# VectorE order, a resident residual and split attention outputs in a one-core hybrid encoder layer

## The chip, the cores and the metric

The kernel runs on one core of a Trainium2 chip. The metric is the device time of one execution, in microseconds (us). The engines are TensorE (PE in the profile, its weight loads PEld), VectorE (DVE), ScalarE (ACT), GpSimd (POOL) and SyncE (SP), whose queue issues nearly all DMAs.

## The reference

One layer of a streaming encoder on 512 prompt frames and 8 x 16 sample frames, 640 tokens of width 1024, in float32:

```python
x = x + 0.5 * swiglu(rmsnorm(x, ffn1_norm), ffn1_wgu, ffn1_wd)      # d_ff 2816
cols = rmsnorm(x, mix_norm) @ w_in
ret_cols, mla_cols, ssm_cols = split(cols)
o_ret = retention(rope(q), rope(k), v) normed, * silu(gate)         # 8 heads of 64
o_mla = latent_attention(c_q 384, c_kv 256, k_rope 32)              # 8 heads, softmax, chunk-causal
o_ssm = rmsnorm((ssd_scan(conv(xbc), dt, a) + d * xs) * silu(z))    # 16 heads of 64, state 128
x = x + concat([o_ret, o_mla, o_ssm]) @ w_out                       # 2048 x 1024
x = x + 0.5 * swiglu(rmsnorm(x, ffn2_norm), ffn2_wgu, ffn2_wd)
```

The sample frames attend to a cache of 256 earlier frames for each of 8 streams (latents `ckv` and a rotary key `krope`), and start from given retention, state-space and convolution states. The outputs are x, the new latents and keys, and the new states.

## The kernel before

Tokens lie on the free axis in five tiles of 128 (`NT` = 5, `T` = 640, `H2` = 320); the 1024 channels are eight tiles of 128 partitions (`NK` = 8). Every large product is done in three passes: each operand is split into a rounded high part (ScalarE's copy to the fast float32 format) and the rest (VectorE's subtraction), and TensorE multiplies high by high, low by high and high by low. `part(h, l, src)` is that split for data (L382, L383); `wunit` splits a loaded weight block `wr` into `wh` (L290) and `wl` (L291).

Stages in order of time: first feed-forward (`ffn("1", ...)`), input projection in units (`tok_first`, `tok_unit`, each with a sink that empties the PSUM bank), attention over the prompt, attention of the samples over the caches (`sample_a` and what follows it), retention and convolution, the state-space scan in five token blocks with the sample steps between, the output projection `wout` in two halves (`woa` for retention and attention, `wos` for the state space), and the second feed-forward. The code is written stage by stage; a scheduler sorts each engine's instructions by priorities (`prio`, and `urgent()` for the highest), and `tc.issue_after` binds an instruction behind another. On each engine the instructions run in the sorted order. SP's DMAs run in its queue's order, so a store that waits holds the loads behind it.

**The feed-forward** multiplies 2 x 2 blocks with seven products in place of eight. For each of four pairs of channel tiles, `blocks(q)` splits the plain blocks and `sums(q)` makes four sums of blocks (L415 to L418) and splits those; `squares(q, eng)` adds the squares of x for the norm (L430). The first two hidden tiles use plain products (L466), the others the seven-product form (L556). `statistics()` turns the squares into the token norms (`norm_stats`, L361, L363) and spreads them into a row tile R (`spread`, L371, L372). R multiplies the gate before and after the silu (`plain_gate` L541, L543; `scaled_silu` L523, L525); L599 is the down projection. In the first feed-forward, `cache_norms` (L682 to L719) prepares the cached keys on the side, with a chain of a reciprocal square root (L265 to L272) at its end.

**Small features.** The unit `winc` makes 176 columns a token: 128 of c_q, 16 of dt and 32 of the rotary key. Its sink (`sink_c`) empties one of two PSUM banks `pd` on two engines: ScalarE takes c_q (L860), VectorE takes dt (`dtr`, L861) and the key (`kr`, L862).

**Attention outputs.** `mix_out` transposes an output tile, copies it to `mo` and stores it in DRAM: `ma_dr` for retention and attention, `ms_dr` for the state space (L920 to L924). Before the output projection `mix_in` loads those as `mraw` and splits them (L1684 to L1687). `sample_a(b)` loads the cached latents of stream b twice, as `c_t` (columns by tokens, L1130) and `c_n` (tokens by columns, L1131), into three buffers.

**Retention** rotates q and k in `ro` with three VectorE instructions (L1286 to L1288) and three GpSimd ones (L1289 to L1291).

**State space.** Decay factors come from a pool with `DECB` = 6 buffers; each block's sample steps load their inputs into `st` and copy them into `sr` (L1616, L1618).

**Output projection.** `sink_x` loads a half row of the residual from `x_dr` into `xc`, adds the PSUM bank (L1701) and stores it to `y_dr`; after the first half all eight rows are loaded again, on GpSimd's queue, into `xres`, to which the second half adds.

Of the kernel before, what the change touches and what calls it, by code (L numbers as in the profile page):

```python
# [197 lines left out]
def body(tc, a):  # L198
# [182 lines left out]
    def part(h, l, src):  # L381
        S.copy(h, src)  # L382
        V.tensor_sub(l, src, h.bitcast(F32))  # L383

    class Tokens:
# [473 lines left out]
    def sink_c(t, ps):  # L859
        S.activation(cqt[:, t, 256:384], ps[:, :128], AF.Copy, scale=rstd[:, t:t + 1])  # L860
        V.scalar_tensor_tensor(dtr[:, t, :], ps[:, 128:144], rstd[:, t:t + 1], rowp[:, R_DTB:R_DTB + 16], op0=ALU.mult, op1=ALU.add)  # L861
        V.tensor_scalar_mul(kr[:, t, :], ps[:, 144:176], rstd[:, t:t + 1])  # L862
# [895 lines left out]
```

## Time and profile before

| | |
|---|---|
| time, median of 3 runs | 1654.43 us (1651.13 to 1659.39) |
| profiled execution | 1650.01 us, span 1648.2 us |
| mean granted TensorE clock | 0.973 |
| busy: TensorE, VectorE, ScalarE, GpSimd | 1603.1, 1128.2, 697.6, 384.0 us |
| DMA | 178.32 MB, 108 GB/s on the mean |

The profile is of one execution, taken by the hardware profiler, and its times count from the first instruction. A row of a timeline gives start, duration, engine, line, operation, output and inputs; a row of a group gives count, busy time and mean in ns. "PEclk" is the clock that TensorE was granted, as a share of full speed. A busy TensorE is not TensorE at full speed: at a clock of 0.5 it is as busy and does half the work.

### The profile page before, as it was taken

To read this page: it belongs to the slowest core of one execution; us is meant where nothing else is said; L and a number is where in the kernel's file an instruction comes from. 1 tells how busy PE (TensorE), PEld (TensorE's weight loads), DVE (VectorE), ACT (ScalarE), POOL (GpSimd) and SP (SyncE) were. 2 spreads that over 40 slices of the span, in tenths; PEclk is the share of its full clock that TensorE was granted. 3 is DMA by queue.
4 is the path that set the end of the run, shared out by engine and by line. 5 is a ranking of instruction groups with operands and counts; after the bars stand their busy time and mean duration, and the time that the engine had idled before them with its cause. 6 is when DMAs were issued, how large, how long until landed. Compare 5 with 4: busy or idle time off the path is not lost.

```text
span 1648.2 us, 27379 instructions
## 1 busy us (share of the span) xinstructions
PE 1603.1 (97%) x10867; PEld 1541.1 (93%) x10867; DVE 1128.2 (68%) x1790; ACT 697.6 (42%) x1282; POOL 384.0 (23%) x396
## 2 busy tenths in 40 slices
PE   8999999999999999999989998999999999999998
PEld 8999999999999999986989996689999999999998
DVE  8788777777573472563689757755678977777762
ACT  6554333333353334553333365433445433343430
POOL 3422222222201000002142224341004422223220
PEclk8999999999997999998999998799999999999999
DMA  4332222222151333113144547677312322222221
GB/s 179 103 94 80 78 88 79 80 87 77 52 203 51 114 99 120 64 42 106 56 146 141 169 144 224 203 235 243 119 46 71 103 77 90 78 79 88 77 77 65
DMA packets 88316, 178.32 MB, mean 108 GB/s; under 512 B 13352, under 2 KB 48072, under 8 KB 87996
## 3 DMA queue, kind: packets, MB, share of 16 engines
q1 hardware_dynamic: 86012, 171.14, 32.9%
q10 hardware_dynamic: 1536, 2.82, 0.6%
q0 software_dynamic: 640, 2.62, 0.5%
q8 instruction: 85, 1.39, 0.4%
q14 instruction: 43, 0.35, 0.1%
HBM read 143.45 MB, written 33.10 MB: 107 GB/s over the span
## 4 chain that ended last, share of the span: by engine, by line
PE 86%; DVE 7%; DMA 4%; issue 2%; ACT 1%; POOL 1%; SPq 0%; DVEq 0%; ACTq 0%; POOLq 0%
PE bank L556 29%; PE pair L599 19%; PE pd L820 12%; PE pd L1662 6%; PE pd L1395 2%; PE pair L466 1%; PE pair L696 1%; PE p L1082 1%; DVE wl L291 1%; PE po L1104 1%; DVE ac L1409 1%; PE pb L1576 1%; PE bank L466 1%; PE ps L1630 1%; DMA mraw<-ms_dr 1%
## 5 line engine op out<-in xcount | busy, mean ns | idle before, releaser
L291 DVE TENSOR_TENSOR wl<-wr,wh 128x1024 fp32r<-128x1024 f32 (+3 forms) x161 | 202.6, 1259 | 52.0 <-ACT wh L290 48.3
L290 ACT CAST wh<-wr 128x1024 fp32r<-128x1024 f32 (+3 forms) x161 | 163.0, 1015 | 171.9 <-PE pair L599 73.3
L599 PE MATMUL pair<-xh,wh 128*128 128x320 f32 x672 | 206.8, 310 | 1.4 <-ACT xh L382 1.0
L599 PE MATMUL pair<-xl,wh 128*128 128x320 f32 x672 | 207.3, 309 | 0.0
L599 PE MATMUL pair<-xh,wl 128*128 128x320 f32 x672 | 207.2, 309 | 0.0
L523 POOL TENSOR_TENSOR gt<-gt,R 128x320 f32<-128x320 f32 x82 | 93.7, 1143 | 481.8 <-DVE gt L583 441.3
L556 PE MATMUL bank<-xsh,wh 128*128 128x320 f32 x656 | 203.0, 310 | 2.3 <-ACT s L560 2.3
L556 PE MATMUL bank<-xsh,wl 128*128 128x320 f32 x656 | 203.3, 310 | 0.0
L556 PE MATMUL bank<-xsl,wh 128*128 128x320 f32 x656 | 203.2, 310 | 0.0
L601 DVE SCALAR_TENSOR_TENSOR x<-pair,x 128x640 f32<-128x640 f32 x96 | 78.7, 822 | 149.9 <-PE pair L599 149.8
L820 PE MATMUL pd<-wh,xh 128*128 128x256 f32 (+1 forms) x560 | 166.5, 297 | 5.3 <-DVE kr L862 3.3
L820 PE MATMUL pd<-wl,xh 128*128 128x256 f32 (+1 forms) x560 | 166.5, 297 | 0.0
L820 PE MATMUL pd<-wh,xl 128*128 128x256 f32 (+1 forms) x560 | 166.2, 297 | 0.0
L525 POOL TENSOR_TENSOR gt<-gt,R 128x320 f32<-128x320 f32 x82 | 118.1, 1442 | 72.6 <-ACT gt L524 72.6
L599 PEld LDWEIGHTS pair<-xh,wh 128*128 128x128 f32 x672 | 125.7, 188 | 2.3 <-ACT xh L382 1.3
L556 PEld LDWEIGHTS bank<-xsh,wh 128*128 128x128 f32 x656 | 123.6, 189 | 3.0 <-ACT s L560 2.6
L599 PEld LDWEIGHTS pair<-xl,wh 128*128 128x128 f32 x672 | 126.2, 188 | 0.1
L599 PEld LDWEIGHTS pair<-xh,wl 128*128 128x128 f32 x672 | 126.1, 188 | 0.0
L556 PEld LDWEIGHTS bank<-xsl,wh 128*128 128x128 f32 x656 | 123.7, 189 | 0.4
L556 PEld LDWEIGHTS bank<-xsh,wl 128*128 128x128 f32 x656 | 123.8, 189 | 0.2
L820 PEld LDWEIGHTS pd<-wh,xh 128*128 128x128 f32 x560 | 112.5, 201 | 8.4 <-issue 5.8
L820 PEld LDWEIGHTS pd<-wl,xh 128*128 128x128 f32 x560 | 112.4, 201 | 3.5 <-issue 3.3
(568 smaller groups left out, 4127.6 us busy)
## 6 DMA issues: line engine op xcount, KB each, us to landing
wr<-in_wgu SPq DMA_DIRECT2D x88, 512.0 KB
wr<-in_wd SPq DMA_DIRECT2D x40, 512.0 KB
wr<-in_wint SPq DMA_DIRECT2D x28, 512.0 KB
wr<-in_winx SPq DMA_DIRECT2D x12, 512.0 KB
qk_dr<-stg SPq DMA_DIRECT2D x40, 128.0 KB
wr<-in_woa SPq DMA_DIRECT2D x8, 512.0 KB
hb<-in_sssm SPq DMA_DIRECT2D x16, 256.0 KB
out_ssms<-hb SPq DMA_DIRECT2D x16, 256.0 KB
```

The lines of the kernel that those rows point to most:

```text
L290: S.copy(hv, raw)
L291: V.tensor_sub(lv, raw, hv.bitcast(F32))
L466: PE.matmul(out[gu][hf], w_, x_, start=q == 0 and k == 0 and i == 0, stop=q == 3 and k == 1 and i == 2)
L523: G.tensor_mul(gt[:, hf], gt[:, hf], R3[:, hf])
L525: G.tensor_mul(gt[:, hf], gt[:, hf], R3[:, hf])
L556: PE.matmul(out, w_[:, o:o + P], x_[:, PSLOT[p]], start=start and k == 0 and i == 0, stop=k == 3 and i == 2, skip_group_check=not start)
L599: PE.matmul(pt[:, hf, :H2], w_[:, o:o + P], x_[:, hf * H2:(hf + 1) * H2], start=j == 0 and i == 0, stop=j == g - 1 and i == 2)
L601: V.scalar_tensor_tensor(xv, pt[:, :, :H2], 0.5, xv, op0=ALU.mult, op1=ALU.add)
L696: PE.matmul(pt[:, kt], x_[:, o:o + P], w_[cc][:, :512], start=c == 0, stop=c == 5)
L820: PE.matmul(ps[:, :w], x_[k][:, t * P:(t + 1) * P], w_[:, k * w:(k + 1) * w], start=c == 0, stop=c == 23)
L1395: PE.matmul(ps[:, :H2], w_[:, o:o + P], x_[k][:, hf * H2:(hf + 1) * H2], start=c == 0, stop=c == 23)
L1662: PE.matmul(ps[:, :H2], w_[:, o:o + P], x_[k][:, hf * H2:(hf + 1) * H2], start=k == 0 and i == 0, stop=k == NK - 1 and i == 2)
```

## The change

1. In the first feed-forward the block work of all four pairs comes first, then all sums, then all squares (bound with `issue_after`); the squares and the plain gates' two products move from GpSimd to VectorE. How many pieces of the previous group's down projection go between the units of the second group becomes 0, 2, 3, 3.
2. `sink_c` empties the bank with one ScalarE copy of 176 columns; one GpSimd copy and one VectorE addition take `kr` and `dtr` from there for all five tiles.
3. The attention outputs are split where they are made (`mix_split`) and stored as two parts (`mh_dr`, `ml_dr`), which are loaded straight into `xh`, `xl`.
4. The first cache uses the buffer that held the keys, and its loads go ahead of the attention stores.
5. Retention's three GpSimd instructions go to VectorE.
6. `sr` is loaded without `st`; `DECB` is 5.
7. The residual is loaded into `xres` before the output projection and stays there; `xc`, `y_dr` and the reload go. R of the mixer, `stg` and `mo` get pools that close at other places.

```diff
             part(h[:, 0], l[:, 0], b1[:, 0])
             part(t[:, 0], t[:, 1], b1[:, 1])
-            part(h[:, 1:3], l[:, 1:3], b2)
+            self.last = part(h[:, 1:3], l[:, 1:3], b2)
...
-            with urgent():
+            with urgent(), tc.issue_after(tok.last.ins):
                 for q in range(4):
-                    tok.squares(q, G)
+                    tok.sums(q)
+            with urgent(), tc.issue_after(tok.last.ins):
+                for q in range(4):
+                    tok.squares(q, V)
...
         def plain_gate(gt, ut):
-            G.tensor_mul(gt, gt, R3)
+            V.tensor_mul(gt, gt, R3)
             S.activation(gt, gt, AF.Silu)
-            G.tensor_mul(gt, gt, R3)
+            V.tensor_mul(gt, gt, R3)
...
-    DECB = 6
+    DECB = 5
...
     def sink_c(t, ps):
-        S.activation(cqt[:, t, 256:384], ps[:, :128], AF.Copy, scale=rstd[:, t:t + 1])
-        V.scalar_tensor_tensor(dtr[:, t, :], ps[:, 128:144], rstd[:, t:t + 1], rowp[:, R_DTB:R_DTB + 16], op0=ALU.mult, op1=ALU.add)
-        V.tensor_scalar_mul(kr[:, t, :], ps[:, 144:176], rstd[:, t:t + 1])
+        S.activation(cqt[:, t, 256:432], ps[:, :176], AF.Copy, scale=rstd[:, t:t + 1])
         S.activation(junk()[:, :128], cqt[:, t, 256:384], AF.Square, accum_out=cqs[:, 1, t:t + 1])
...
+    G.tensor_copy(kr, cqt[:, :, 400:432])
+    V.tensor_add(dtr, cqt[:, :, 384:400], brow(rowp[:, R_DTB:R_DTB + 16], NT))
...
+    def mix_split(src, k0, n, t, where):
+        pt = turn()
+        for i in range(n):
+            PE.transpose(pt[:, i * P:(i + 1) * P], src[:, i * P:(i + 1) * P], ident)
+        h, l = (where.tile([P, n, P], F32R, tag=s, name=nm(s), bufs=2) for s in ("moh", "mol"))
+        pv = pt[:, :n * P].rearrange("p (f t) -> p f t", f=n)
+        S.copy(h, pv)
+        V.tensor_sub(l, pv, h.bitcast(F32))
+        Q.dma_start(out=mh_dr[:, k0:k0 + n, t * P:(t + 1) * P], in_=h.bitcast(F32))
+        Q.dma_start(out=ml_dr[:, k0:k0 + n, t * P:(t + 1) * P], in_=l.bitcast(F32))
...
         def sample_a(b):
-            c_t = t1_.tile([P, 2, 272], F32, tag="c_t", name=nm("c_t"), bufs=3)
-            c_n = t1_.tile([P, 2, CKV], F32, tag="c_n", name=nm("c_n"), bufs=3)
+            if b == 0:
+                kt_ = m0.tile([P, 1600], F32, tag="K", name=nm("K"))
+                c_t, c_n = kt_[:, 0:544].rearrange("p (c n) -> p c n", c=2), kt_[:, 544:1056].rearrange("p (c n) -> p c n", c=2)
...
-        G.tensor_mul(ro[:, :, 32:64], x1, sn)
-        G.tensor_mul(tb, x2, cs)
-        G.tensor_add(ro[:, :, 32:64], ro[:, :, 32:64], tb)
+        V.tensor_mul(ro[:, :, 32:64], x1, sn)
+        V.tensor_mul(tb, x2, cs)
+        V.tensor_add(ro[:, :, 32:64], ro[:, :, 32:64], tb)
...
         def sample_load(b):
-            st = sb.tile([P, 1280], F32, tag="st", name=nm("st"), bufs=STKB)
+            sr[0] = sb.tile([P, 1280], F32R, tag="sr", name=nm("sr"), bufs=SRB)
             for o in range(2):
-                Q.dma_start(out=st[64 * o:64 * o + 64], in_=xw_dr[b + o])
-            sr[0] = sb.tile([P, 1280], F32R, tag="sr", name=nm("sr"), bufs=SRB)
-            S.copy(sr[0], st)
+                Q.dma_start(out=sr[0][64 * o:64 * o + 64].bitcast(F32), in_=xw_dr[b + o])
...
+    xres = [None] * NK
+    for k in range(NK):
+        xres[k] = x2p.tile([P, T], F32, tag=f"x{k}", name=nm("x2"))
+        Q.dma_start(out=xres[k], in_=x_dr[k])
...
     def sink_x(d, cs, ps):
-        xc = wp.tile([P, H2], F32, tag="xc", name=nm("xc"))
-        Q.dma_start(out=xc, in_=x_dr[d][:, cs])
-        V.tensor_add(xc, ps, xc)
-        Q.dma_start(out=y_dr[d][:, cs], in_=xc)
+        V.tensor_add(xres[d][:, cs], ps, xres[d][:, cs])
```

VectorE at the opening, before. `xh_26` is the first pair's lower tile, `xh_29` the second pair's; L383 splits a block, L400 scales a tile, L415 to L418 are sums, L291 splits weights.

```order
L415 TENSOR_TENSOR xh_26_171<-xh_26_171 128x320
L400 TENSOR_SCALAR xh_27_172<-x_5_105,colp 128x640
L291 TENSOR_TENSOR wl_151<-wr_148,wh_150 128x1024
L416 TENSOR_TENSOR xh_26_171<-xh_26_171,xh_27_172 128x320
L383 TENSOR_TENSOR xsl_118<-xh_27_172,xsh_119 128x640
L291 TENSOR_TENSOR wl_158<-wr_155,wh_157 128x1024
L400 TENSOR_SCALAR xh_30_183<-x_6_106,colp 128x640
L417 TENSOR_TENSOR xh_27_172<-xh_27_172,xh_26_171 128x320
L383 TENSOR_TENSOR xsl_118<-xh_26_171,xsh_119 128x640
L400 TENSOR_SCALAR xh_33_194<-x_7_107,colp 128x640
L418 TENSOR_TENSOR xh_27_172<-xh_27_172 128x320
L383 TENSOR_TENSOR xsl_116<-xh_29_182,xsh_117 128x320
```

After, with its own line numbers (L381 splits, L398 scales, L413 is the first sum, L289 splits weights):

```order
L381 TENSOR_TENSOR xsl_115<-xh_29_182,xsh_116 128x320
L381 TENSOR_TENSOR xl_31_186<-xh_29_182,xl_31_186 128x320
L398 TENSOR_SCALAR xh_33_194<-x_7_106,colp 128x640
L381 TENSOR_TENSOR xsl_115<-xh_30_183,xsh_116 128x640
L381 TENSOR_TENSOR xsl_113<-xh_32_193,xsh_114 128x320
L398 TENSOR_SCALAR xh_36_205<-x_8_107,colp 128x640
L381 TENSOR_TENSOR xl_34_197<-xh_32_193,xl_34_197 128x320
L381 TENSOR_TENSOR xsl_113<-xh_33_194,xsh_114 128x640
L381 TENSOR_TENSOR xsl_111<-xh_35_204,xsh_112 128x320
L381 TENSOR_TENSOR xl_37_208<-xh_35_204,xl_37_208 128x320
L381 TENSOR_TENSOR xsl_111<-xh_36_205,xsh_112 128x640
L413 TENSOR_TENSOR xh_26_171<-xh_26_171 128x320
```

Before, the four sums of the first pair stand between its blocks and those of the second; after, the first sum comes behind the blocks of the fourth.

VectorE around the end of the cache keys' chain (`ivc` is its result) and the small features, before (`pd` are the PSUM banks):

```order
L291 TENSOR_TENSOR wl_5435<-wr_5432,wh_5434 128x1024
L272 SCALAR_TENSOR_TENSOR ivc<-rit_5406,riy_5404 128x128
L861 SCALAR_TENSOR_TENSOR dtr<-pd_5048,rstd,rowp 128x16
L862 TENSOR_SCALAR kr<-pd_5048,rstd 128x32
L861 SCALAR_TENSOR_TENSOR dtr<-pd_5078,rstd,rowp 128x16
L862 TENSOR_SCALAR kr<-pd_5078,rstd 128x32
```

After:

```order
L268 TENSOR_TENSOR rit_5405<-rit_5405,rih_5404 128x128
L289 TENSOR_TENSOR wl_5434<-wr_5431,wh_5433 128x1024
L270 SCALAR_TENSOR_TENSOR ivc<-rit_5405,riy_5403 128x128
L289 TENSOR_TENSOR wl_5440<-wr_5437,wh_5439 128x1024
L289 TENSOR_TENSOR wl_5586<-wr_5583,wh_5585 128x1024
L873 TENSOR_TENSOR dtr<-cqt,rowp 128x80
L875 TENSOR_TENSOR cqs<-cqs 128x5
```

No instruction that empties a `pd` bank of this unit stands behind the chain any more. ScalarE, which now empties them alone (L862):

```order
L859 ACTIVATE jnk_5041,cqs<-cqt 128x256
L862 ACTIVATE cqt<-pd_5055,rstd 128x176
L863 ACTIVATE jnk_5081,cqs<-cqt 128x128
L862 ACTIVATE cqt<-pd_5083,rstd 128x176
L863 ACTIVATE jnk_5109,cqs<-cqt 128x128
```

SP's queue at the start of the samples' attention, before:

```order
L924 DMA ma_dr<-mo_6857 128x2x128
L924 DMA ma_dr<-mo_6917 128x2x128
L924 DMA ma_dr<-mo_6985 128x2x128
L924 DMA ma_dr<-mo_7061 128x2x128
L1130 DMA c_t_7133<-in_ckvT 128x2x256
L924 DMA ma_dr<-mo_7122 128x2x128
L1131 DMA c_n_7134<-in_ckvN 128x512
L1130 DMA c_t_7167<-in_ckvT 128x2x256
L1131 DMA c_n_7168<-in_ckvN 128x512
```

After:

```order
L891 DMA qk_dr_4829<-stg_8456 128x256
L1150 DMA K_7156<-in_ckvT 128x2x256
L1151 DMA K_7156<-in_ckvN 128x512
L936 DMA mh_dr<-moh_6632 128x2x128
L937 DMA ml_dr<-mol_6633 128x2x128
```

and further on in the same queue:

```order
L936 DMA mh_dr<-moh_7078 128x2x128
L937 DMA ml_dr<-mol_7079 128x2x128
L936 DMA mh_dr<-moh_7142 128x2x128
L937 DMA ml_dr<-mol_7143 128x2x128
L1150 DMA c_t_7187<-in_ckvT 128x2x256
L1151 DMA c_n_7188<-in_ckvN 128x512
```

The first cache (now in buffer `K`) stands ahead of all attention stores, the second behind all sixteen; before, the first stood ahead of the last of eight and the second behind it.

On TensorE the instructions are the same in number and shape; 373 matmuls instead of 326 (the warm-up's left out) stand ahead of the first L599, and 396 of the output projection's 768 instead of 506 behind the last transposes of the state-space stage.

More of the change, by code (lines that the diff above doesn't have):

```diff
@@ L419, in sums @@
             part(h[:, 3:5], l[:, 3:5], b1)
-            part(h[:, 5:7], l[:, 5:7], b2)
+            self.last = part(h[:, 5:7], l[:, 5:7], b2)
         def squares(self, q, eng):
@@ L615, in ffn @@
             acts = []
-            per = 8 // g
             for j in range(g):
+                per = (0, 2, 3, 3)[j] if first and gi == 1 else 8 // g
                 if f < npl:
@@ L621, in ffn @@
                         uts = [plain_gate(*u) for u in raw_out]
-                        with urgent():
-                            for q in range(4):
-                                tok.sums(q)
                         for i in range(2):
@@ L723, in body @@
     with ExitStack() as st:
+        r1 = pool(st, "R1", side="right")
         xp = pool(st, "x1", side="right")
@@ L728, in body @@
         tok.open((0, 1, 2, 3))
-        ffn("1", tok, True, False, bank, pair, R)
+        ffn("1", tok, True, False, bank, pair, r1.tile([P, T], F32, tag="R", name="R"))
         prio(10)
@@ L784, in body @@
     stg_st = ExitStack()
-    stg = pool(stg_st, "stg", 4)
+    stg = pool(stg_st, "stg", 4, side="right")
+    R_st = ExitStack()
+    R = pool(R_st, "Rm", side="right").tile([P, T], F32, tag="R", name="Rm")
     dtr = keep.tile([P, NT, SH], F32, tag="dtr", name="dtr")
@@ L795, in body @@
     xs_dr = [tc.dram_tile([P, 1024], F32, name=f"xs_dr{t}") for t in range(NT)]
-    ma_dr = tc.dram_tile([P, NK, T], F32, name="ma_dr")
+    ma_dr = tc.dram_tile([P, 4, T], F32, name="ma_dr")
+    mh_dr, ml_dr = (tc.dram_tile([P, 4, T], F32, name=n) for n in ("mh_dr", "ml_dr"))
     MSC = (0, 384, T)
@@ L852, in body @@
     t0 = pool(mt_st, "mt0")
-    cqt = t0.tile([P, NT, CQ], F32, tag="cqt", name="cqt")
+    cqt = t0.tile([P, NT, CQ + 48], F32, tag="cqt", name="cqt")
     def sink_a(t, ps):
@@ L945, in body @@
         for t in range(NT):
-            cq = cqt[:, t, :]
+            cq = cqt[:, t, 0:CQ]
             S.activation(cq, cq, AF.Copy, scale=cqr[:, t:t + 1])
@@ L1048, in prep @@
         def prep(u):
-            K = ub.tile([P, 16, 96], F32, tag="K", name=nm("K"))
+            K = m0.tile([P, 1600], F32, tag="K", name=nm("K"))[:, 0:1536].rearrange("p (a d) -> p a d", a=16)
             Vv = ub.tile([P, 4, 256], F32, tag="Vv", name=nm("Vv"), bufs=2)
@@ L1193, in body @@
         ret_unit(u)
+    for u in range(ZPRE):
+        tok_unit(a["wint"][2 + u], 256, silu_sink(z_dr, 256 * u))
+    mog_st = ExitStack()
+    mog = pool(mog_st, "mog", 2)
     ssd_st = ExitStack()
@@ L1469, in body @@
         tok_unit(a["wint"][2 + u], 256, silu_sink(z_dr, 256 * u))
+    stg_st.close()
+    x2p = pool(x2_st, "x2", side="right")
     wo_st = ExitStack()
     wp = pool(wo_st, "wop", MRAWB, side="right")
-    y_dr = [tc.dram_tile([P, T], F32, name=f"y_dr{k}") for k in range(NK)]
     prio(17)
@@ L1682, in mix_in @@
         h, l = xh[k][:, cs], xl[k][:, cs]
-        raw = wp.tile([P, 384], F32, tag="mraw", name=nm("mraw"))[:, 0:c1 - c0]
+        raw = wp.tile([P, c1 - c0], F32, tag="mraw", name=nm("mraw"))
         Q.dma_start(out=raw, in_=src)
```

39 lines of the change are left out of this document (20 added, 19 removed).

## The prediction, made before the changed kernel was run

> **What bounds the kernel now.** I read the page first, for the engine that sets the time and the chain that ended last.
>
> ```profile
> PE 1603.1 (97%) x10867; PEld 1541.1 (93%) x10867; DVE 1128.2 (68%) x1790; ACT 697.6 (42%) x1282; POOL 384.0 (23%) x396
> PE 86%; DVE 7%; DMA 4%; issue 2%; ACT 1%; POOL 1%; SPq 0%; DVEq 0%; ACTq 0%; POOLq 0%
> ```
>
> TensorE is busy for 97% of the span and holds 86% of the chain. The change leaves its matmuls as they are (in number and shape), so nothing can come from less TensorE work. What can go is TensorE's idle time (1648.2 - 1603.1 = 45 us) and time in which it is "busy" at a lower granted clock (PEclk, 1.00 is full). Next the span cut by stage, which shows where both sit.
>
> ```profile
> core 0: us, PE busy (x) PEld busy (x) DVE busy (x) ACT busy (x) POOL busy (x), PEclk, DMA share, GB/s
> 0.00:74.00 74.00, 65.01 (x380) 62.77 (x381) 62.24 (x78) 45.40 (x72) 33.15 (x35) 0.91 0.43 150
> 74.00:456.00 382.00, 382.00 (x2556) 378.12 (x2554) 280.24 (x343) 154.26 (x244) 98.60 (x78) 1.00 0.26 79
> 500.00:530.00 30.00, 26.99 (x154) 27.02 (x155) 9.87 (x31) 9.31 (x25) 3.16 (x9) 0.66 0.22 69
> 750.00:800.00 50.00, 44.92 (x261) 34.46 (x261) 22.08 (x72) 14.03 (x53) 9.20 (x48) 0.90 0.31 91
> 845.00:860.00 15.00, 11.37 (x92) 11.00 (x91) 13.14 (x17) 3.91 (x7) 3.83 (x9) 0.89 0.38 110
> 985.00:1080.00 95.00, 84.76 (x411) 66.87 (x410) 72.35 (x122) 45.94 (x96) 37.92 (x24) 0.80 0.68 212
> 1135.00:1155.00 20.00, 17.46 (x109) 17.20 (x108) 9.96 (x18) 7.82 (x14) 2.13 (x4) 0.91 0.97 306
> ```
>
> From 74 to 456 us TensorE has no gap and full clock: 382.00 / 2556 = 0.149 us a matmul, my unit below. The first feed-forward holds nothing to gain behind its opening. Six stretches have gaps and a clock under 1: the opening, 500 to 530, 750 to 800, 845 to 860, the state-space stage (985 to 1080), and 1135 to 1155. Then who TensorE waits for (us in total, times, longest).
>
> ```profile
> PE pa L1297 <- DVE ro L1288: 4.4, 2, 3.6
> PE pair L466 <- DVE xsl L383: 3.9, 3, 2.1
> PE pd L820 <- DVE kr L862: 3.3, 1, 3.3
> PE pa L1535 <- DVE stm L1530: 2.9, 1, 2.9
> PE pb L1576 <- DVE yi L1556: 2.8, 1, 2.8
> PE pd L1662 <- DVE xc L1701: 2.5, 1, 2.5
> PE bank L556 <- ACT s L560: 2.3, 1, 2.3
> PE p L1145 <- DMA c_t<-in_ckvT: 1.8, 1, 1.8
> ```
>
> These are single waits of 2 to 4 us, most of them on VectorE, and the change touches nearly all of them.
>
> **1. Opening: block work in fixed order, no GpSimd.** Rows of VectorE, TensorE, and of the two forms of the squares:
>
> ```profile
> 8.94 1.85 DVE L416 TENSOR_TENSOR xh<-xh,xh 128x320 f32<-128x320 f32 x1
> 22.83 0.48 DVE L416 TENSOR_TENSOR xh<-xh,xh 128x320 f32<-128x320 f32 x1
> 43.28 0.16 DVE L363 TENSOR_SCALAR nv<-pair 128x5 f32<-128x5 f32 x1
> 8.39 0.39 PE L466 MATMUL pair<-xsh,wh 128*128 128x320 f32 x1
> 72.56 0.31 PE L599 MATMUL pair<-xh,wh 128*128 128x320 f32 x1
> L430 DVE TENSOR_TENSOR xl<-xl,xl 128x640 f32<-128x640 f32 x7 | 5.7, 819 | 4.6 <-ACT xl L429 4.6
> L430 POOL TENSOR_TENSOR xl<-xl,xl 128x640 f32<-128x640 f32 x7 | 13.8, 1974 | 16.2 <-ACT xl L429 16.1
> ```
>
> Before, 326 matmuls lie between the first of the opening (8.39) and the first of the down projection (72.56). At 0.149 us they need 48.6 us; 64.2 passed, so 15.6 us were lost. The cause is VectorE, full until the statistics (43.28): the same addition takes 1.85 us while one of GpSimd's seven squares runs and 0.48 us otherwise, and it alternates blocks and sums, so TensorE waits for the next block. The change does the blocks of all four pairs first and drops the seven GpSimd squares; some eight to nine stretched instructions go, at 1.85 - 0.48 = 1.37 us each, about 12 us. It adds to VectorE seven squares of 0.82 us (5.7) and, behind the statistics, four gate products of the same size (3.3) that GpSimd did. By the order, 373 matmuls instead of 326 now lie ahead of the first down projection, 47 x 0.149 = 7.0 us of work done earlier. I sum VectorE's 67 new rows up to the statistics at undisturbed durations to 42 us, so to 48 us; TensorE reaches its 276th matmul, the statistics, at 8.4 + 276 x 0.149 = 49.5, balanced, plus a short start in which it outruns the blocks. The way from the statistics to the first down projection took 72.6 - 43.3 = 29 us and holds four GpSimd products of the squares' size, 1.97 us, now 0.82: about 22 to 24 us. So the first down projection comes at 70 to 72, and the gain is 72.6 - 71 + 7.0 = 9, between 6 and 12. The far bounds: 15.6 (all loss gone), and -3, if one more wait like that of L556 on L560 (2.3 us) comes. I take **-9**. The cover of the added VectorE work is the time freed of GpSimd; without it they would cost 9.
>
> **2. Small features leave VectorE (winc).** VectorE, then TensorE in 5 us windows:
>
> ```profile
> 502.28 0.28 DVE L272 SCALAR_TENSOR_TENSOR ivc<-rit,riy 128x128 f32<-128x128 f32 x1
> 502.48 0.22 DVE L861 SCALAR_TENSOR_TENSOR dtr<-pd,rstd,rowp 128x16 f32<-128x16 f32 x1
> 495.00:500.00 5.00, 4.72 (x37) 4.05 (x35) 4.76 (x11) 2.76 (x11) 3.36 (x6) 1.00 0.00 0
> 500.00:505.00 5.00, 1.99 (x10) 2.02 (x10) 3.16 (x8) 0.24 (x1) 0.00 (x0) 0.69 0.52 163
> 505.00:510.00 5.00, 5.00 (x25) 5.00 (x25) 0.39 (x2) 0.77 (x3) 0.00 (x0) 0.50 0.13 50
> 525.00:530.00 5.00, 5.00 (x44) 5.00 (x43) 0.00 (x0) 3.79 (x10) 0.06 (x1) 1.00 0.01 3
> L860 ACT ACTIVATE cqt<-pd,rstd 128x128 f32<-128x128 f32 x5 | 1.8, 366 | 14.6 <-PE pd L820 14.6
> ```
>
> L861 and L862 empty TensorE's two accumulators, but stand behind the cache keys' chain, which ends with L272 at 502.3; TensorE waits 3.3 us. Then the clock is 0.50, with 25 matmuls in 5 us against 44; the mean of 0.66 from 500 to 530 makes 30 x 0.34 x 2 = 20 us of it. From 500 to 530 there are 154 matmuls; at 44 in 5 us they need 17.5 us, so 12.5 of the 30 are lost. In the new kernel one ScalarE copy of 176 columns (bounded by the 0.37 of 128, about 0.42) empties the bank. Ahead of it on ScalarE stands nothing of that chain; its added time is 5 x 0.05. The copy of kr moves to GpSimd and dtr to one VectorE instruction, behind the last tile; the krope store starts later, and nothing here waits for it. Bounds: -13 and -3.3 (wait alone goes). I take **-12**, as both wait and clock are in the rows.
>
> By the Trainium skill, "TensorE: Matmul & The Clock Gate" (Part 1: The HAM clock gate), the clock halves after an idle window of about 3.4 us and returns after about as much busy time; an estimate from that is 3.3 + 1.7 = 5 us for this event. The trace differs: 20 us of busy matmuls stay at 0.50. By the page the sum would be 7 us weaker.
>
> **3. First cache early, outputs in two parts.**
>
> ```profile
> 751.45 0.56 SPq L1130 DMA_DIRECT2D c_t<-in_ckvT  x1
> 753.73 0.56 SPq L1130 DMA_DIRECT2D c_t<-in_ckvT  x1
> 754.63 2.15 PE L1145 MATMUL p<-c_t,qab 128*128 128x272 f32 x4 [1.83 <-DMA c_t<-in_ckvT]
> ```
>
> The first cache is issued at 751.45, and its data are there 3.2 us later. It now goes ahead of the attention stores on SP, so that wait goes. But the second cache stands behind the last two of 16 stores (before 8), and was issued at 753.7: with the same 3.2 us it lands at 757, while TensorE needs it after the first cache's six matmuls, 1.7 us at full clock (half of the 3.3 that pass at the halved one), so at 754.5. So most of the wait moves to the second cache. The subtraction (0.48 us, as a 128x320 row) and the store (as long an issue as the load's 0.56) that each output has more lie beside TensorE's work, except the last. Bounds: -5 (1.8, and of the low clock, 50 x 0.10 = 5 us, some 3) and +3. I take **-2**.
>
> **4. Retention's rotation from GpSimd to VectorE.**
>
> ```profile
> L1287 DVE TENSOR_TENSOR ta<-qk,cst 128x512 f32<-128x512 f32 x5 | 5.6, 1119 | 0.7 <-DMA qk<-qk_dr 0.7
> L1288 DVE TENSOR_TENSOR ro<-ro,ta 128x512 f32<-128x512 f32 x5 | 3.4, 681 | 0.0
> L1290 POOL TENSOR_TENSOR tb<-qk,cst 128x512 f32<-128x512 f32 x5 | 8.5, 1709 | 11.5 <-DMA qk<-qk_dr 11.5
> ```
>
> Three GpSimd instructions a block, of up to 1.7 us, become three on VectorE of 0.68, undisturbed as L1288: +2.0 us a block there. Two or three VectorE instructions a block lose their stretch of up to 1.1 us (L1287 shows 1.12 on the mean): -2 to -3. VectorE's load stays the same; the result is no longer late by GpSimd. The wait of 3.6 us on L1288, and the low clock behind it (15 x 0.11 = 1.7 us), shorten. Bounds: -5, and +3 if VectorE, 88% busy from 845 to 860, queues the rotation behind the convolution. I take **-3**.
>
> **5. State-space stage and output projection.**
>
> ```profile
> L1687 DVE TENSOR_TENSOR xl<-mraw,xh 128x320 fp32r<-128x320 f32 x8 | 6.0, 763 | 0.0
> L1701 DVE TENSOR_TENSOR xc<-pd,xc 128x320 f32<-128x320 f32 x16 | 7.8, 486 | 6.9 <-DMA xc<-x_dr 3.9 <-PE pd L1662 2.9
> ```
>
> From 985 to 1080 TensorE idles 10.2 us and the clock is 0.80, 19 us of clock: up to 29 us could go. The change takes from this stage eight VectorE splits (6.0 us; the attention half arrives as two parts), their eight ScalarE casts and four casts of the sample states, and puts 110 matmuls of the output projection more between the steps: 396 instead of 506 follow the stage's last transposes. These are 110 x 0.149 = 16 us of cover for the same gaps. Against that stands one decay buffer less (5 for 6), so the next block's decays can only start later. Bounds: -16 and +13 (one event like that of 500). I take **-8**, half the cover. The residual in SBUF removes the wait on L1701 (2.5 and 1.8 of clock in 1135 to 1155): -4. But the 396 matmuls that follow are not all free: only some 60 need no state-space output, 9 us of cover for the store, the reload and the split. The load of the first cache alone took 3.2 us from its issue, a store and a reload 6.4, and the splits of eight parts 6 us on VectorE; I put +3 for a new wait there, so **-1** for the two, between -4 and +6. FFN2's inputs now need no reload: 0, since its opening is covered by the same matmuls.
>
> **Sum.** -9 - 12 - 2 - 3 - 8 - 1 = -35. The profiled execution took 1650.0 (span 1648.2), so it would take 1615. The median of the runs is 4.4 above it, so I forecast **1619**, a ratio of 0.979; its own range is 1605 to 1633.
>
> **Rivals.** A change of under 0.5% (8.3 us) can't be told from none.
> - *The low clock after 503 isn't from the wait.* If narrow matmuls (176 columns) make it, the wait goes and the clock stays: 3.3 instead of 12, so 1628. For: 20 us is long for a wait of 3.3. Against: from 495 to 500, with the same narrow matmuls, the clock is 1.00. Chance 0.12.
> - *Waits only move.* The first down projection waits for the gates as before (opening -3), the second cache (0), the state-space chain stays as it is (0), a new wait before the state-space half of the output projection eats L1701's: -15 in all with the 12 of step 2, 1639. For: the chain of the state-space stage is one of dependent steps on VectorE. Chance 0.18.
> - *The change does little.* As the last, and step 2's queue is replaced by one on ScalarE: 1650. For: ScalarE also splits weights in that stretch. Chance 0.08.
> - *Slower.* With five decay buffers each of the four later blocks of the state-space stage waits for a free one, and each wait brings the low clock: 3.3 + 9 = 12 us as at 503, four times 48, against 35 gained: 1667. It decides from four such events. For: that stage already has 0.80. Against: VectorE gets 6 us and GpSimd is not loaded further. Chance 0.04.
>
> **How the numbers follow.** The forecast holds 0.58. Faster by over 0.5% (under 1646): 0.58 + 0.12 + 0.18, less 0.02 for the upper end of the third = 0.86; the same: 0.08 + 0.02 = 0.10; slower 0.04. The range reaches from the forecast's lower end, opened to 1602 by the bounds of steps 1 and 5, to 1645, which takes in the waits that only move.
>
> **What would show it.** Right: the first down projection near 71 with 373 matmuls ahead and no GpSimd work before the statistics; no wait on L862 and a clock of 1.0 from 500 to 530; the wait for the cache at its second load; fewer than 5 us of wait on the rotation; a clock above 0.85 in the state-space stage. Wrong: VectorE at or above 95% there, a wait of over 3 us on the gates, or any new stretch of 10 us at 0.50.

## The result, and the profile after

The changed kernel took 1628.27 us (median of 4 runs, 1626.21 to 1631.61) against 1654.09 of the kernel before (4 runs): a ratio of 0.984, 95% interval 0.981 to 0.988, about 26 us less. A second set of runs (e5) gave 1628.75 and 0.986 (0.983 to 0.988). The forecast was 1619, with a range of 1602 to 1645. The profiled execution took 1630.27 us with a span of 1628.5, 19.7 less than the profiled one before; the traces explain those 19.7, and the other 6 are the distance of the two profiled executions from their medians (4.1 below and 2.0 above).

The page of the changed kernel, busy times and the chain:

```profile
PE 1592.4 (98%) x10867; PEld 1528.8 (94%) x10867; DVE 1120.2 (69%) x1810; ACT 690.9 (42%) x1270; POOL 332.9 (20%) x361
PE 87%; DMA 5%; DVE 4%; ACT 2%; issue 1%; POOL 1%; SPq 0%; ACTq 0%; DVEq 0%; POOLq 0%
```

TensorE has the same 10867 instructions; VectorE's share of the chain fell from 7% to 4%, DMA's rose from 4% to 5%. The stretches that answer to those of before (same columns):

```profile
0.00:74.00 74.00, 66.84 (x420) 62.86 (x420) 60.18 (x91) 47.92 (x75) 12.05 (x25) 1.00 0.46 153
482.00:512.00 30.00, 29.94 (x253) 29.46 (x253) 18.82 (x45) 17.77 (x50) 12.11 (x20) 1.00 0.30 98
602.00:632.00 30.00, 28.58 (x211) 27.56 (x210) 2.68 (x3) 12.49 (x38) 0.00 (x0) 0.89 0.39 110
735.00:785.00 50.00, 45.36 (x269) 35.40 (x268) 23.03 (x73) 14.73 (x53) 8.87 (x47) 0.90 0.28 83
830.00:845.00 15.00, 15.00 (x127) 14.35 (x127) 15.00 (x27) 7.61 (x13) 3.58 (x9) 1.00 0.33 99
965.00:1060.00 95.00, 88.43 (x471) 71.78 (x469) 67.15 (x118) 40.78 (x82) 39.56 (x23) 0.84 0.72 234
```

The opening holds 420 matmuls in 74 us (380 before), the stretch of the small features 253 in 30 us at full clock (154 before at 0.66), and retention has neither a gap nor a low clock. The samples' attention and the state-space stage look as before: 0.90, and 0.84 after 0.80. A new low stretch lies at 602 to 632; in the second profile of the same kernel (e5) that stretch has 1.00. TensorE's waits:

```profile
PE ps L1655 <- DMA sr<-xw_dr: 7.0, 2, 4.4
PE pd L1683 <- ACT xh L1710: 2.1, 2, 1.5
PE pd L1683 <- DVE xl L1711: 2.1, 2, 1.4
PE pair L694 <- ACT gt L697: 1.7, 1, 1.7
PE pair L369 <- DVE xl L366: 1.7, 2, 1.5
PE p L1163 <- DMA c_t<-in_ckvT: 1.7, 1, 1.7
PE bank L557 <- DVE ut L582: 1.5, 1, 1.5
PE px L1030 <- DMA wukT<-in_wukT: 1.4, 1, 1.4
PE pair L694 <- ACT R L370: 1.3, 1, 1.3
```

Of the eight waits shown of before, those on `xsl`, `kr`, `ro`, `stm`, `yi`, `xc` and `s` are gone or under 1 us, and the one on `c_t` is the second cache's now. The longest new one is on `sr`, the sample inputs of the state-space stage, which come back from DRAM.

Where the 19.7 us came from, by the start of the same matmul in both traces (us; lines of the kernel before):

| matmul | before | after | gained so far | in this stage |
|---|---|---|---|---|
| first of the small features (L820) | 493.1 | 487.1 | 6.0 | 6.0 opening |
| first transpose of the latents (L940) | 543.3 | 524.9 | 18.4 | 12.4 small features |
| behind `wukT` (L1027) | 646.9 | 631.5 | 15.4 | -3.0 |
| last of the samples' attention (L1182) | 797.0 | 782.2 | 14.8 | -0.6 |
| last of retention's blocks (L1323) | 925.5 | 904.5 | 21.0 | 6.2 |
| last of the output projection (L1662) | 1211.6 | 1192.6 | 19.0 | -2.0 sample retention, state space and output projection |
| last of all (L599) | 1643.9 | 1624.2 | 19.7 | 0.7 second feed-forward |

### The profile page after: what moved, and what is told of

It reads as the page before. It is cut to its first block, busy times and chain, and to the rows that moved or that the text cites. A ratio compares the mean times of both kernels' runs of the same rounds, so it can differ in the third digit from the quotient of the medians.

```text
span 1628.5 us, 27264 instructions
## 1 busy us (share of the span) xinstructions
PE 1592.4 (98%) x10867; PEld 1528.8 (94%) x10867; DVE 1120.2 (69%) x1810; ACT 690.9 (42%) x1270; POOL 332.9 (20%) x361
## 4 chain that ended last, share of the span: by engine, by line
PE 87%; DMA 5%; DVE 4%; ACT 2%; issue 1%; POOL 1%; SPq 0%; ACTq 0%; DVEq 0%; POOLq 0%
PE bank L557 30%; PE pair L600 18%; PE pd L822 11%; PE pd L1683 7%; PE pd L1417 5%; PE pair L464 2%; PE pair L694 1%; PE p L1095 1%; PE po L1117 1%; PE bank L464 1%; PE pb L1599 1%; PE ps L1651 1%; DVE wl L289 1%; DMA xw_dr<-z 1%; DMA sr<-xw_dr 1%
## 5 line engine op out<-in xcount | busy, mean ns | idle before, releaser
L289 DVE TENSOR_TENSOR wl<-wr,wh 128x1024 fp32r<-128x1024 f32 (+3 forms) x161 | 198.5, 1234 | 55.6 <-ACT wh L288 50.6
L557 PE MATMUL bank<-xsh,wh 128*128 128x320 f32 x656 | 203.0, 310 | 1.6 <-DVE ut L582 1.5
L557 PE MATMUL bank<-xsl,wh 128*128 128x320 f32 x656 | 202.5, 309 | 0.0
L557 PE MATMUL bank<-xsh,wl 128*128 128x320 f32 x656 | 202.5, 309 | 0.0
L524 POOL TENSOR_TENSOR gt<-gt,R 128x320 f32<-128x320 f32 x82 | 93.7, 1143 | 481.5 <-DVE gt L584 427.7
L822 PE MATMUL pd<-wh,xl 128*128 128x256 f32 (+1 forms) x560 | 161.7, 289 | 0.0
L526 POOL TENSOR_TENSOR gt<-gt,R 128x320 f32<-128x320 f32 x82 | 113.8, 1388 | 74.5 <-ACT gt L525 74.5
L557 PEld LDWEIGHTS bank<-xsh,wh 128*128 128x128 f32 x656 | 123.3, 188 | 2.9 <-DVE ut L582 2.1
L557 PEld LDWEIGHTS bank<-xsl,wh 128*128 128x128 f32 x656 | 123.3, 188 | 0.3
L557 PEld LDWEIGHTS bank<-xsh,wl 128*128 128x128 f32 x656 | 123.3, 188 | 0.1
L822 PEld LDWEIGHTS pd<-wh,xl 128*128 128x128 f32 x560 | 109.6, 196 | 1.8 <-issue 1.6
```

The source lines that it names most:

```text
L289: V.tensor_sub(lv, raw, hv.bitcast(F32))
L524: G.tensor_mul(gt[:, hf], gt[:, hf], R3[:, hf])
L526: G.tensor_mul(gt[:, hf], gt[:, hf], R3[:, hf])
L557: PE.matmul(out, w_[:, o:o + P], x_[:, PSLOT[p]], start=start and k == 0 and i == 0, stop=k == 3 and i == 2, skip_group_check=not start)
L822: PE.matmul(ps[:, :w], x_[k][:, t * P:(t + 1) * P], w_[:, k * w:(k + 1) * w], start=c == 0, stop=c == 23)
```

## The experiments

Ratios are to the kernel before, runs of which stand among each set. For e1 to e4 and e10 the gains in us are worked out from the recorded ratio, whose interval is given; by the medians of all runs they are 9.9 (e1), 6.5 (e2), 2.4 (e3), 2.9 (e4) and 5.8 (e10). The variants of the changed kernel (e6 to e8, e12) are compared with it by medians. What is said of a stage comes from one profiled execution of a kernel.

**e1: the small features alone.** In the kernel before:

```diff
     def sink_c(t, ps):
-        S.activation(cqt[:, t, 256:384], ps[:, :128], AF.Copy, scale=rstd[:, t:t + 1])
-        V.scalar_tensor_tensor(dtr[:, t, :], ps[:, 128:144], ...)
-        V.tensor_scalar_mul(kr[:, t, :], ps[:, 144:176], rstd[:, t:t + 1])
+        S.activation(cqt[:, t, 256:432], ps[:, :176], AF.Copy, scale=rstd[:, t:t + 1])
...
+    G.tensor_copy(kr, cqt[:, :, 400:432])
+    V.tensor_add(dtr, cqt[:, :, 384:400], brow(rowp[:, R_DTB:R_DTB + 16], NT))
```

> The kernel before with only the small features' sink of the change (one ScalarE copy of 176 columns, then one GpSimd copy and one VectorE addition). Theory: the wait of 3.3 us on L862 and the 20 us of halved clock behind it go together, about -12 us (1654 to 1642), and no window from 490 to 530 shows a clock under 1. Rival: the narrow matmuls make the low clock, the wait alone goes: -3.3 us, and 25 matmuls in 5 us stay.

1642.33 us, ratio 0.9925 (0.990 to 0.995): -12.4 us of 1652, with 8 to 17 inside the interval. Windows of this kernel:

```profile
500.00:505.00 5.00, 5.00 (x48) 5.00 (x46) 1.48 (x3) 2.56 (x7) 0.00 (x0) 1.00 0.67 202
500.00:530.00 30.00, 30.00 (x252) 29.68 (x251) 15.12 (x44) 14.57 (x36) 4.24 (x10) 1.00 0.34 108
```

Without the wait the same 176-column matmuls run at full clock, 252 in the 30 us that held 154. The rival that narrow matmuls make the low clock by themselves falls.

**e10: why one wait of 3.3 us cost 12.** The kernel before with wider matmuls in that unit and nothing else:

```diff
-                    PE.matmul(ps[:, :w], x_[k][:, t * P:(t + 1) * P], w_[:, k * w:(k + 1) * w], ...)
+                    n = wide if wide and k % 4 < 3 else w
+                    PE.matmul(ps[:, :n], x_[k][:, t * P:(t + 1) * P], w_[:, k * w:k * w + n], ...)
...
-    tok_unit(a["winc"], 176, sink_c)
+    tok_unit(a["winc"], 176, sink_c, wide=256)
```

> The kernel before with 18 of 24 matmuls a tile of the winc unit made 256 columns wide in place of 176 (the 80 more are weights of the next channel tile, and nothing reads their sums); the order of all instructions is the same. At full clock this costs 90 x 0.009 = 0.8 us. Theory: the wait of 3.3 us on L862 stays, but the low clock behind it ends some 4 us after it and not 20 us, since it ends only under dense matmuls: -5 to -8 us, 500 to 530 at a mean clock over 0.85. Rival: the low clock there lasts whatever is fed: 0 to +2 us, mean clock 0.66.

1646.72 us, ratio 0.998 (0.996 to 1.000): -3.5 us. Its wait and windows:

```profile
PE pd L821 <- DVE kr L863: 2.9, 1, 2.9
500.00:505.00 5.00, 3.23 (x20) 3.26 (x21) 1.93 (x6) 0.00 (x0) 0.00 (x0) 0.80 0.67 209
505.00:510.00 5.00, 5.00 (x39) 5.00 (x39) 0.79 (x4) 1.54 (x6) 0.00 (x0) 0.86 0.01 4
510.00:515.00 5.00, 5.00 (x45) 5.00 (x44) 3.19 (x7) 2.88 (x6) 0.36 (x1) 1.00 0.21 61
500.00:530.00 30.00, 28.23 (x224) 28.26 (x225) 12.22 (x38) 13.54 (x33) 3.18 (x9) 0.94 0.27 78
```

The wait is still there (2.9 us), and more columns are computed, but the clock is back before 510: 30 x 0.06 x 2 = 3.6 us of half clock in place of 20. In the profile 70 matmuls more stand in the 30 us, some 8 us of work. The whole run gains less than that, and less than the 5 to 8 us expected, though its interval leaves up to 6.6. The trace shows where the rest went: it is 9.6 us ahead of the kernel before at the first transposes of the state-space stage and 5.9 at the last matmul of the output projection.

**e9: the clock by itself.** Behind the end of the changed kernel, 60 dense matmuls between blocks of one kind (`phase(n, x, rows, cols)` is n matmuls, `gap` a VectorE chain whose result the next matmuls wait for):

```diff
+        phase(60, ar, P, 320)
+        phase(90, a32, P, 64)
+        phase(60, ar, P, 320)
+        phase(24, ar, 26, 512)
...
+        r = gap(p, 3)
+        phase(100, ar, P, 176, r)
+        p = phase(60, ar, P, 512)
+        r = gap(p, 3)
+        phase(80, ar, P, 256, r)
...
```

> The changed kernel with some 130 us of TensorE work put behind its end, on data already there, whose results nothing uses: dense matmuls of 320 columns between blocks of one kind (64 columns of plain float32, as in the state-space stage; 26 rows by 512 columns; 512 columns of plain float32; 176 columns), and then, behind an idle time of some 3 us made by a VectorE chain, 100 matmuls of 176 columns, 80 of 256 and 60 of 320. Only its profile is read. Theory: the granted clock follows how densely TensorE is fed and not only waits: it falls to 0.5 without a wait in one of the sparse blocks (64 columns, or 26 rows), and behind an idle time it stays at 0.5 over all 100 matmuls of 176 columns but returns within 3 to 5 us with 256 or 320. Rival: only waits lower it: 1.0 in all blocks without a wait, and the same time to return behind each idle time.

Windows cut at the blocks: 64 columns; 26 rows; the dense ones behind them; 176 columns; then, each behind a wait of 4.3 to 4.5 us, 176 columns (two windows), 256 columns (two) and 320 (two):

```profile
1643.00:1653.20 10.20, 10.20 (x94) 10.20 (x93) 0.00 (x0) 0.00 (x0) 0.00 (x0) 1.00 0.01 2
1662.10:1668.20 6.10, 6.10 (x25) 4.39 (x24) 0.00 (x0) 0.00 (x0) 0.00 (x0) 0.93 0.00 0
1668.20:1679.70 11.50, 11.50 (x61) 11.50 (x61) 0.00 (x0) 0.00 (x0) 0.00 (x0) 0.74 0.00 0
1709.20:1719.20 10.00, 10.00 (x91) 10.00 (x91) 0.00 (x0) 0.00 (x0) 0.00 (x0) 1.00 0.01 2
1737.30:1747.30 10.00, 9.95 (x47) 9.95 (x47) 0.00 (x0) 0.00 (x1) 0.00 (x0) 0.50 0.01 2
1747.30:1758.70 11.40, 11.40 (x55) 11.40 (x55) 0.00 (x0) 0.00 (x0) 0.00 (x0) 0.50 0.00 0
1779.00:1784.00 5.00, 4.99 (x25) 4.99 (x26) 0.00 (x0) 0.00 (x0) 0.00 (x0) 0.56 0.01 3
1784.00:1790.60 6.60, 6.60 (x57) 6.60 (x56) 0.00 (x0) 0.00 (x0) 0.00 (x0) 1.00 0.00 0
1808.90:1814.00 5.10, 5.10 (x19) 5.10 (x20) 0.00 (x0) 0.00 (x0) 0.00 (x0) 0.50 0.01 3
1814.00:1821.00 7.00, 6.30 (x43) 6.04 (x41) 0.49 (x1) 0.00 (x0) 0.00 (x0) 0.99 0.00 0
```

176 columns keep a full clock (1.00) but don't bring it back: all 100 of them behind a wait, 21.4 us, stay at 0.50. 256 columns bring it back in 5 x 0.44 x 2 = 4.4 us, 320 in about 5.1. And matmuls of 26 rows lower the clock with no wait at all: TensorE is busy throughout, and from the end of that block on there are some 6.1 x 0.07 x 2 + 11.5 x 0.26 x 2 = 6.8 us of half clock. The 64 columns of the state-space stage's form don't do so.

This is one profile, but the kernel before shows the same of 176 and 256 columns: behind its wait, 72 matmuls of 176 columns run from 503.0 to 518.6 at 0.50, matmuls of 256 follow, and the clock comes back 4 us later (0.50 from 515 to 520, 0.76 from 520 to 525).

The rule of the Trainium skill, "TensorE: Matmul & The Clock Gate" (Part 1: The HAM clock gate), that some 3.4 us of sustained work release the clock, agrees roughly with 4.4 and 5.1 us for wide matmuls; for 176 columns the trace differs.

**e2: the opening alone.** The kernel before with the first item of the change (its lines stand in the diff above).

> The kernel before with only the opening of the first feed-forward changed (blocks, then sums, then squares, all on VectorE; plain gates on VectorE; the pieces 0, 2, 3, 3). Theory: as the two profiles' loss up to the first down projection (18.8 us before, 12.8 after), -6 us, with new short waits between 65 and 75 us on the gates' and cached keys' work. Rival of the prediction: -9 us. Rival: the new waits eat it, 0 +- 2.

1645.74 us, ratio 0.995 (0.993 to 0.997): -8.2 us. The changed kernel's waits on L369, L694, L557 come back in it under its own line numbers:

```profile
PE pair L696 <- ACT gt L699: 1.7, 1, 1.7
PE bank L559 <- DVE ut L584: 1.5, 1, 1.5
PE pair L371 <- DVE xl L368: 1.4, 2, 1.2
PE pair L696 <- ACT R L372: 1.3, 1, 1.3
```

In its trace the first matmul of the small features comes 6.0 us earlier, as in the changed kernel. The interval of the whole run (5 to 11 us) doesn't tell the theory's 6 from the prediction's 9.

**e3: the sample inputs loaded directly, alone.**

```diff
-            st = sb.tile([P, 1280], F32, tag="st", name=nm("st"), bufs=STKB)
+            sr[0] = sb.tile([P, 1280], F32R, tag="sr", name=nm("sr"), bufs=SRB)
             for o in range(2):
-                Q.dma_start(out=st[64 * o:64 * o + 64], in_=xw_dr[b + o])
-            sr[0] = sb.tile([P, 1280], F32R, tag="sr", name=nm("sr"), bufs=SRB)
-            S.copy(sr[0], st)
+                Q.dma_start(out=sr[0][64 * o:64 * o + 64].bitcast(F32), in_=xw_dr[b + o])
```

> The kernel before with only the sample inputs loaded straight into sr (no st, no ScalarE copy). Theory: sr has one buffer, so a load can be issued only behind the last use of the one before and stands in SP's queue behind the state loads; new waits on the load of 2 to 4 us each, with low clock behind them: +3 to +10 us. Rival: the copies of 4 x 1.26 us leave the path, and the waits in the changed kernel come from its other order: 0 to -4 us.

1649.77 us, ratio 0.997 (0.995 to 0.999): -5.1 us, and TensorE waited 0.2 us on `sr` in all. My theory fell: the single buffer does no harm in the kernel before. That the wait in the changed kernel comes with its other order and earlier start is what is left, not shown by a run.

**e4: retention's rotation on VectorE, alone.**

```diff
-        G.tensor_mul(ro[:, :, 32:64], x1, sn)
-        G.tensor_mul(tb, x2, cs)
-        G.tensor_add(ro[:, :, 32:64], ro[:, :, 32:64], tb)
+        V.tensor_mul(ro[:, :, 32:64], x1, sn)
+        V.tensor_mul(tb, x2, cs)
+        V.tensor_add(ro[:, :, 32:64], ro[:, :, 32:64], tb)
```

> The kernel before with only retention's three GpSimd instructions a block on VectorE. Theory: the waits on L1288 (4.4 us) and the stretch of VectorE's own instructions go: -6 us, as the two profiles' difference from 797 to 925 us (17.5 us of loss before, 8.1 after). Rival of the prediction: -3 us. Rival: VectorE becomes the bound there (full from 845 to 860): 0 to +3 us.

1649.30 us, ratio 0.998 (0.996 to 1.001): -2.6 us, not told from none. The longest wait and two windows of this kernel:

```profile
PE ps L1634 <- ACT sr L1618: 8.1, 1, 8.1
...
800.00:875.00 75.00, 74.31 (x553) 72.59 (x552) 67.76 (x124) 31.99 (x46) 16.70 (x36) 1.00 0.42 137
960.00:1060.00 100.00, 87.49 (x451) 70.67 (x449) 65.22 (x106) 51.56 (x105) 41.07 (x24) 0.78 0.67 203
```

The kernel before had 69.50 and 505 matmuls in the first, 89.76 at 0.89 in the second. The stage gains what was expected: 48 matmuls more in 75 us, about 7 us. The state-space stage gives most of it back: TensorE comes to the first sample step earlier and waits 8.1 us for `sr`.

That is no matter of this run alone. By the traces the lead on the kernel before, at the first transposes of the state-space stage and then at the last matmul of the output projection, is 9.2 and 3.1 us in e4, 15.0 and 10.4 in e1, 10.6 and 5.6 in e2. Some of it may be scatter between executions: e11, which has only one buffer less and comes 0.9 us earlier, falls 3.0 behind.

**e8: the changed kernel with the rotation back on GpSimd** (e4's diff the other way), beside **e5**, the changed kernel again.

> The changed kernel with retention's three instructions a block back on GpSimd. Theory: the waits on the rotation come back (some 4 us, with low clock behind them 6 us), but the state-space stage then starts later and waits less on the sample inputs: +2 to +5 us against the changed kernel. Rival, from the stage alone: +6 us or more. Rival: no difference, 0 +- 2 us.

1644.28 us (1643.33 to 1645.16) against 1628.75 (1627.83 to 1632.44): +15.5 us. The theory (+2 to +5) fell; the rival's "+6 us or more" holds, by far more than the 6 it was worked out from. The waits of e8:

```profile
PE pb L1599 <- DVE state L1589: 4.7, 3, 3.1
PE pa L1319 <- DVE ro L1310: 3.8, 2, 3.0
...
PE pd L1417 <- DVE pre L1420: 3.0, 1, 3.0
PE pa L1558 <- DVE stm L1553: 2.9, 1, 2.9
```

The waits on the rotation (3.8) are back, as expected, and with them one on the convolution (3.0). By the traces of e5 and e8, 7 us are lost in retention and 10 more in the state-space stage and the output projection, with waits on the state and its decays, where the order of the instructions changed too. Why this larger part comes there is open.

**e6: the sample inputs' preparation first.**

```diff
-        cur = ssd_a(0)
         sample_pre()
+        cur = ssd_a(0)
```

> The changed kernel with the sample inputs' preparation ahead of the first block's decay work (two lines swapped), so that their stores to DRAM and the first load back stand earlier on each queue; nothing is left out. Theory: the state-space stage is held by that round trip through DRAM (store 11.6 us, load 4.2 us to landing), so the expected gain of that stage was given back there; the wait of 4.4 us at the first sr and low clock behind it go, -4 to -10 us against the changed kernel. Rival: the chain of dependent VectorE and GpSimd steps holds the stage; the wait goes and another one of the same size comes on the decay work that is now behind: 0 +- 3 us.

 

> The changed kernel again, as the measure for the three beside it on the same chip. Both theories: 1626 to 1632 us, with the wait on the sample inputs (sr) of some 4 us near 1001 us and of 2 to 3 us near 1095 us.

1629.14 us against 1628.75: no difference, though with four runs from 1623.69 to 1634.85 a few us either way can't be told. In e5 the waits on `sr` were 8.6 us (the longest 7.6; 4.4 in the first profile of the same kernel); in e6 they are gone, and others stand in their place:

```profile
PE pd L1683 <- DVE x L1728: 3.4, 1, 3.4
PE ps L1655 <- DVE hb L1656: 2.6, 1, 2.6
PE pb L1599 <- DVE state L1589: 2.5, 1, 2.5
PE ps L1651 <- DMA hb<-in_sssm: 1.9, 1, 1.9
965.00:1060.00 95.00, 89.64 (x446) 70.05 (x446) 70.18 (x129) 41.50 (x89) 41.44 (x25) 0.78 0.71 232
```

The theory's -4 to -10 did not come, and the rival fits: the round trip through DRAM is the last wait of the stage, and not its only one.

**e7: `sr` in halves.** One lasting buffer, both halves loaded at the start and each again behind its last use:

```diff
...
+            if b + 2 < 8:
+                sample_load(b + 2)
```

> The changed kernel with sr as one lasting buffer whose halves are loaded sample by sample, two samples ahead, instead of pairwise behind the last use of both halves. Theory that the single buffer makes the second wait: the wait of 2.6 us near 1095 goes, the first (4.4 us) stays: -3 to -6 us against the changed kernel. Rival (the state loads hb in front of it on SP's queue make it): 0 +- 2 us.

1632.45 us against 1628.75, intervals of the ratios 0.984 to 0.990 and 0.983 to 0.988: no gain where 3 to 6 us were expected. The second wait went, the first was 6.9 us.

**e11: five decay buffers alone.** `DECB = 5` in the kernel before.

> The kernel before with five decay buffers in place of six. Theory: the buffer isn't what ate the state-space stage's gain: 0 +- 3 us. Rival (the prediction's slower case): each block waits for a free one, +8 us or more, with new waits of TensorE on the decay work (dec, stm).

1652.78 us, ratio 0.999 (0.997 to 1.001): no difference.

**e12: more rows.** The changed kernel with 38 rows of zeros more in each of the state-space stage's 20 matmuls of 26 rows:

```diff
-                PE.matmul(pt, L[o:o + 26, b0:b0 + P], Rr[o:o + 26, ...], start=True, stop=True)
+                PE.matmul(pt, L[o:o + 64, b0:b0 + P], Rr[o:o + 64, ...], start=True, stop=True)
```

> The changed kernel with the 20 matmuls of 26 rows in the state-space stage (L1558) fed with 64 rows, of which 38 are zeros; two GpSimd memsets more ahead of the stage, and the order of everything else is the same. Theory: these sparse matmuls lower the granted clock in that stage without a wait (as 24 of them in a row did by themselves), which no part of the change touches; with more rows the clock falls less often, -4 to -12 us against the changed kernel's 1628.5 and a mean clock over 0.90 from 965 to 1060 (0.84 before). Rival: rows of zeros count for nothing, or the stage's low clock comes from its waits and its other short matmuls: 0 +- 3 us, clock 0.84.

1631.18 us (5 runs), ratio 0.988 (0.985 to 0.990), against 1628.3 and 1628.8 of the changed kernel: no gain; 4 to 12 us were expected. The mean clock from 965 to 1060 is 0.86, against 0.84 of the changed kernel and the 0.90 expected. Its windows do differ. The changed kernel, then e12:

```profile
965.00:975.00 10.00, 10.00 (x65) 8.71 (x64) 4.15 (x9) 3.46 (x6) 1.90 (x1) 0.84 0.71 228
975.00:985.00 10.00, 10.00 (x49) 8.30 (x48) 9.18 (x9) 4.15 (x9) 6.95 (x4) 0.63 0.42 118
```

```profile
965.00:975.00 10.00, 10.00 (x65) 8.11 (x65) 4.23 (x5) 5.69 (x10) 3.72 (x2) 1.00 0.69 225
975.00:985.00 10.00, 7.96 (x53) 6.57 (x53) 6.87 (x8) 2.99 (x8) 5.71 (x4) 1.00 0.51 160
985.00:995.00 10.00, 5.57 (x30) 3.62 (x28) 8.59 (x23) 6.65 (x14) 0.00 (x0) 1.00 0.62 178
995.00:1005.00 10.00, 6.79 (x29) 6.36 (x30) 5.18 (x5) 1.18 (x4) 9.12 (x5) 0.50 0.98 322
```

In the changed kernel TensorE has no gap from 965 to 985 and yet runs 10 us at half clock; in e12 that low stretch is gone, the time appears as waits from 975 to 1000 (6.3 us of them on `sr`), and another low stretch follows. So the stage is not held by TensorE's clock from 965 to 985. The second profile of the changed kernel (e5) has the same 10 us of half clock there without a gap; e12 has one profile. That the 26 rows make the low stretch in the stage is likely by e9 and e12, not shown beyond them.

## Why the prediction was right, and where it was off

The sign, the size and the range held: -35 in the sum, -20 in the trace and -26 in the medians. The mechanism held for the small features and the rotation, in part for the opening, and not for the state-space stage. That the total came so close is partly luck: the rotation gave 3 us more than its price, which made up for some of what the state-space stage failed to give. The first rival's 1628, to which the measured 1628.27 comes closest, agrees by chance: e1 refutes its cause.

1. *Opening, -9.* -6.0 in the trace, as in that of e2, whose runs give -8.2; inside the bounds. The mis-sized term is the time of the statistics. I put them at 48, where VectorE's rows end, though by my own count TensorE reaches its matmuls for them only at 49.5. It began them at 50.4, and VectorE's row came at 51.66:

```profile
51.66 0.17 DVE L361 TENSOR_SCALAR nv<-pair 128x5 f32<-128x5 f32 x1
```

From there to the first down projection, at 74.8 and not at 71, passed 23.2 us, as forecast (22 to 24), with waits of 1.3 to 1.7 us on R, the gates and the cached keys' work in them.
2. *Small features, -12.* -12.4 in the trace; alone (e1) -12.6 in this stage of the trace and -12.4 by the runs' ratio. The mechanism, wait and clock together, is shown; the rival with 0.12 fell. What I could not say, why the clock stays low for 20 us, is shown by e9 and e10: 176 columns don't bring it back.
3. *First cache, -2.* The wait moved to the second cache (1.7 us), and nothing was left of the gain: the stage lost 0.6. My working gave no gain either: data at 757 that are needed at 754.5 are a wait of 2.5 us, longer than the 1.8 that goes. A wait not in the prediction came ahead of it, 1.4 us for `wukT`, whose load now stands 4.3 us ahead of the first matmul that could use it and took 5.7. With a low clock behind it, it cost 3.0 us in this execution; in e5's profile the wait is 1.0 and the clock stays at 1.00.
4. *Rotation, -3.* -6.2 in its stage, where VectorE was 88% busy and is now full without making TensorE wait. Alone it is given back in the state-space stage (e4); in the change it is worth 15.5 (e8), 7 of them in this stage.
5. *State space and output projection, -8 and -1.* This step failed: the two lost 2.0, and 1.2 in e5's profile. I priced 110 more matmuls at half their 16 us, as cover for the stage's gaps. They did not fill the gaps:

| from the stage's first transposes to its last product (L1576) | before | after |
|---|---|---|
| time, us | 156.5 | 172.9 |
| TensorE idle in it, us | 10.2 | 10.7 |
| mean granted clock in it | 0.88 | 0.87 |
| output projection's matmuls in its chain, us | 31.2 | 49.9 |
| time from there to the last of the output projection, us | 89.5 | 75.2 |

The stage grew by 16.4 us, all the time of the 110 matmuls, and what follows shrank by 14.3. The chain that ended last holds 18.7 us more of them (12 in e5), so most of them ran where TensorE's work was the chain already. Where it isn't, from 956.7 to 1000.7, the chain goes through the other engines and DRAM (start, us):

```profile
977.73 6.57 DMA z_dr<-stg
985.38 10.93 DMA xw_dr<-z
996.37 4.25 DMA sr<-xw_dr
```

`xw_dr` and `sr` are the sample inputs' store and load: by SP's waits the load waited last for that store, 3.2 us, and TensorE has it at 1000.7 (1000.6 in e5). But with that wait gone (e6), with loads in halves (e7) or without the low stretch ahead of it (e12) the kernel takes as long, and five decay buffers cost nothing in the kernel before (e11). Which chain would be last if all of these were gone was not tried, so what holds the stage stays open. The wait on `xc` went as forecast, and new waits on the state-space half's split (L1710, L1711: 4.2 us) took its place, as the +3 said.

The rival "waits only move" described the first cache and the state-space stage well; it was wrong for the opening and the rotation. The slower case did not come. Of the signs named beforehand, these came: no wait on L862 and a full clock from 500 to 530, the wait at the second cache, no wait on the rotation, 47 more matmuls ahead of the first down projection. The clock of the state-space stage, 0.84, missed its 0.85, and one sign of being wrong came: 10 us more at half clock, between 965 and 985.

## What to carry to other kernels

Price a wait by what TensorE does behind it: if narrow or short matmuls follow, a wait of 3 us can cost 12, and widening those matmuls takes a part of it back without removing the wait. Count work put between dependent steps as cover only where you can name the wait that it fills: here 110 matmuls made the stage longer by their own time and left its waits. A gain at one place can be spent at the next fixed arrival: ask what will be waited for when everything ahead comes 20 us earlier.

## What was not expected of the hardware

In e9 the granted clock fell to 0.5 with TensorE busy throughout, behind 24 matmuls of 26 rows (about 6.8 us of half clock), and it stayed at 0.5 over 21.4 us of busy 176-column matmuls, while 256 columns brought it back in 4.4 us. So "busy" in the profile is not what releases the clock. In the kernel before, that made 20 us of half clock out of a wait of 3.3 us.
